# Rotary embedding by heads: a later first store, later reloads, and two-row products on GpSimd

## The chip, the core and the metric

The kernel runs on one core of one Trainium2 chip. The metric is device time in microseconds (us): the median of several executions. One more execution is taken with the hardware profiler; its rows carry every duration used below.

## The reference, cut to what matters

```python
x: (16, 512, 1024) fp32 -> reshape (batch, seq, 16 heads, 64)
x1, x2 = x[..., :32], x[..., 32:]
rotated = concatenate([x1 * cos - x2 * sin, x1 * sin + x2 * cos], axis=-1)   # cos, sin: (512, 32)
```

The input is 33.6 MB and the output is 33.6 MB; each element of x is read once and each element of the result is written once.

## The kernel before

**Rows and tiles.** One "row" is 128 partitions by 1024 fp32 elements (16 heads of 64), that is 0.5 MB. The work has 64 rows, numbered u = 0 to 63, in ten tiles: tiles 0 and 1 of four rows, tiles 2 to 7 of eight rows, tiles 8 and 9 of four rows. A tile is loaded by one DMA and stored by one DMA. With four rows a partition's piece of it is 16 KB in one stretch, with eight rows 32 KB.

**Per row.** out = x·[cos, cos] + swap(x)·[−sin, sin], where swap exchanges the two halves of every head. The first product, t1, is made by VectorE into PSUM (`mul`, L293; three buffers, `NT1`). The second, t2, is made by GpSimd into SBUF (L257; six buffers, `NT2`). For row 3 of each eight-row tile (`V2`) VectorE makes t2 too (L286). The sum goes back over x in SBUF. VectorE makes it (`comb`, L304) for most rows. For the rows in `PE2` (21 of 64: rows 1, 3 and 6 of an eight-row tile, one or two in the four-row tiles) TensorE adds t2 to t1 in PSUM by a product with the identity (L224), and ScalarE copies the sum to x (L191).

**Order.** Every engine's program is written out by hand, in row order. VectorE's loop does `mul(u)` and then `comb(u-1)`. At one place, the test called `ahead`, it does `comb(u-1)` first: before, at u = 4, so that the sum of row 3 (the last of tile 0) comes before the product of row 4. A `mul` waits until the t1 buffer of row u−3 is free; GpSimd waits until the t2 buffer of row u−6 is free.

**Transfers.** x has a ring of 40 rows (`RING`). ScalarE's queue issues all loads (L153): those of tiles 0 to 5 at once, at the start. Tiles 6, 7 and the pair 8 and 9 reuse ring places. Each waits on ScalarE for the store that empties its place (`sem_out`), and stands in ScalarE's program behind a certain row: behind row 7 + `LAG` = 17 for tile 6, row 25 for tile 7, row 33 for tiles 8 and 9. While ScalarE waits there it can't copy any sum. SyncE issues the stores (L161) in tile order, each after `wait_added` for the tile's last row: all VectorE sums and ScalarE copies up to that row.

Of the kernel before, what the change touches and what calls it, by code (L numbers as in the profile page):

```python
# [6 lines left out]
def bass_split_heads_rope_kernel(  # L7
# [17 lines left out]
    H = int(num_heads)  # L25
    HD = dim // H
    HALF = HD // 2
    P = 128
    R1 = seq // P
    R2 = 2 * R1  # L30
# [4 lines left out]
    mult = mybir.AluOpType.mult  # L35
# [5 lines left out]
    tiles = [(b, R1 if b in singles else R2) for b in range(batch) if b in singles or b % 2 == 0]  # L41
# [3 lines left out]
    rows = [(t, r) for t, (_, n) in enumerate(tiles) for r in range(n)]  # L45
    NU = len(rows)
# [1 line left out]


    V_ROW = 3  # L50
    PE2 = [R1 <= u < NU - R1 and u % R2 in (1, 3, 6) for u in range(NU)]
    V2 = [tiles[t][1] == R2 and r == V_ROW for t, r in rows]

    def count(flags):
        return [sum(flags[: u + 1]) for u in range(NU)]

    n_pool = count([not v for v in V2])
    n_pe = count(PE2)
    n_comb = count([not a for a in PE2])

    NT1 = 3
    NT2 = 6
    BANK = 512
    EH = H * HD // BANK
    LEAD = 1
    LAG = 10

    with ExitStack() as stack:
        x_sb = stack.enter_context(nc.sbuf_tensor([P, RING, H, 2, HALF], fp32))
        t2_sb = stack.enter_context(nc.sbuf_tensor([P, NT2, H, 2, HALF], fp32))  # L70
        stage = stack.enter_context(nc.sbuf_tensor([P, 2, R1 * HALF], fp32))
        s1_sb = stack.enter_context(nc.sbuf_tensor([P, R1, 2, HALF], fp32))
        s2_sb = stack.enter_context(nc.sbuf_tensor([P, R2, 2, HALF], fp32))
# [16 lines left out]
        sem_p = stack.enter_context(nc.semaphore("pool"))  # L90
# [10 lines left out]
        def c_of(t, r):  # L101
            return c1_ps[:, r, :] if tiles[t][1] == R1 else pair_ps[:, r // R1, 0, r % R1, :]

        def s_of(t, r):
            return s1_sb[:, r] if tiles[t][1] == R1 else s2_sb[:, r]
# [7 lines left out]
        def in_dram(single, pairs, t):  # L113
            b, n = tiles[t]
            return single[b] if n == R1 else pairs[b // 2]

        def in_sbuf(t):
            b, n = tiles[t]
            k = b * R1 % RING
            return x_sb[:, k:k + n].rearrange("p n h t d -> p (n h t d)")  # L120

        def where(u):
            t, r = rows[u]
            return t, r, u % RING

        def swapped(k):
            return x_sb[:, k, :, ::-1, :]

        def over_heads(table):
            return table[:, None, :, :].broadcast_to([P, H, 2, HALF])  # L130

        def wait_added(eng, u):

            if n_pe[u]:
                eng.wait_ge(sem_a, n_pe[u])
            if n_comb[u]:
                eng.wait_ge(sem_v, n_comb[u])  # L137

        def wait_t2_free(eng, u):

            if u >= NT2:
                v = u - NT2
                if PE2[v]:
                    eng.wait_ge(sem_e, n_pe[v])
                else:
                    eng.wait_ge(sem_v, n_comb[v])

        def stores_of(k):

            return sum(b * R1 // R2 == k for b, _ in tiles)  # L150
# [4 lines left out]
        def on_sync(sp):  # L155
            for u in range(NU):
                t, r, k = where(u)
                if r == tiles[t][1] - 1:
                    wait_added(sp, u)
                    k = u // R2  # L160
                    sp.dma_start(in_dram(o1, o2, t), in_sbuf(t)).then_inc(sem_out[k] if k < EARLY else sem_rest, 16)  # L161
            sp.wait_ge(sem_rest, 16 * sum(stores_of(k) for k in range(EARLY, NU // R2)))

        def on_scalar(ae):
            later = {}
            for t, (b, n) in enumerate(tiles):
                if b * R1 + n <= RING:
                    load(ae, t)
                else:

                    later.setdefault((b * R1 - RING) // R2 * R2 + R2 - 1 + LAG, []).append(t)
                if t == 0:
# [15 lines left out]
            for u in range(NU):  # L188
                if PE2[u]:
                    ae.wait_ge(sem_e, n_pe[u])  # L190
# [6 lines left out]
        def on_tensor(pe):  # L197
# [17 lines left out]
            for u in range(NU):  # L215
                if not PE2[u]:
                    continue
# [16 lines left out]
        def on_gpsimd(pl):  # L234
            pl.memset(ident[:], 1.0).then_inc(sem_i, 1)  # L235
            pl.wait_ge(sem_i, 1)
            pl.affine_select(  # L237
                out=ident[:],
                in_=ident[:],
                compare_op=mybir.AluOpType.is_equal,  # L240
                fill=0.0,
                base=0,
                pattern=[[-1, P]],
                channel_multiplier=1,
            ).then_inc(sem_i, 1)
            for u in range(NU):
                if V2[u]:
                    continue
                t, r, k = where(u)
                if (t, r) == (0, 0):  # L250
                    pl.wait_ge(sem_s, 1)
                if (t, r) == (2, 0):
                    pl.wait_ge(sem_s, 2)
                if r == 0:
                    pl.wait_ge(sem_in[t], 16)
                wait_t2_free(pl, u)
                pl.tensor_tensor(  # L257
                    t2_sb[:, u % NT2, :, :, :], swapped(k), over_heads(s_of(t, r)), mult
                ).then_inc(sem_p, 1)

        def on_vector(ve):
            ve.memset(zero[:], 0.0).then_inc(sem_z, 1)  # L262
            ve.wait_ge(sem_cos, 16)
            ve.tensor_copy(c1_ps, stage[:, 0, :].rearrange("s (r d) -> s r d", d=HALF)).then_inc(sem_c, 1)  # L264
            ve.wait_ge(sem_c, 1)
            ve.wait_ge(sem_w, NT1 * EH)

            def pair_tables():
                ve.wait_ge(sem_s, 2)
                row = pair_ps[:, V_ROW // R1, 1, V_ROW % R1, :]  # L270
                ve.tensor_scalar_mul(v_ps[:, 0, :], row, -1.0).then_inc(sem_c, 1)
                ve.tensor_copy(v_ps[:, 1, :], row).then_inc(sem_c, 1)

            first_v = V2.index(True)

            def mul(u):
                t, r, k = where(u)
                if r == 0:
                    ve.wait_ge(sem_in[t], 16)
                if (t, r) == (2, 0):  # L280
                    pair_tables()
                if u == first_v:
                    ve.wait_ge(sem_c, 3)
                if V2[u]:
                    wait_t2_free(ve, u)
                    ve.tensor_tensor(t2_sb[:, u % NT2, :, :, :], swapped(k), over_heads(v_ps), mult)  # L286
                if u >= NT1:
                    v = u - NT1
                    if PE2[v]:
                        ve.wait_ge(sem_a, n_pe[v])  # L290
                    else:
                        ve.wait_ge(sem_v, n_comb[v])
                ve.tensor_tensor(  # L293
                    t1_ps[:, u % NT1, :].rearrange("p (h d) -> p h d", d=HALF),
                    x_sb[:, k, :, :, :].rearrange("p h t d -> p (h t) d"),
                    c_of(t, r)[:, None, :].broadcast_to([P, 2 * H, HALF]),
                    mult,
                ).then_inc(sem_m, 1)

            def comb(u):  # L300
                t, r, k = where(u)
                ve.wait_ge(sem_m, u + 1)
                ve.wait_ge(sem_p, n_pool[u])  # L303
                ve.tensor_tensor(  # L304
                    xs[:, k, :],
                    t1_ps[:, u % NT1, :],
                    t2_sb[:, u % NT2, :, :, :].rearrange("p h t d -> p (h t d)"),
                    add,
                ).then_inc(sem_v, 1)

            for u in range(NU + LEAD):

                ahead = u == R1
                if ahead:
                    comb(u - LEAD)
                if u < NU:
                    mul(u)
                if u >= LEAD and not ahead and not PE2[u - LEAD]:
                    comb(u - LEAD)

        on_sync(nc.sync)
        on_scalar(nc.scalar)
        on_gpsimd(nc.gpsimd)
        on_tensor(nc.tensor)
        on_vector(nc.vector)


# [31 lines left out]
```

## Time and profile before

| what | value |
|---|---|
| median of 3 runs | 161.26 us (161.24 to 161.27) |
| profiled execution, its own time | 161.16 us |
| its span in the profile | 159.8 us |
| DMA traffic in it | 67.26 MB, mean 421 GB/s |
| GpSimd busy | 134.9 us (84%), 58 products of 2350 ns |
| VectorE busy | 130.1 us (81%) |
| TensorE busy / ScalarE busy | 70.4 us / 24.4 us |

The page gives the busy time of each engine, the span in 40 slices, the DMA queues (q10 carries the loads, q1 the stores), the chain of work that ended last, and groups of instructions by line. Program names appear without their numbers: `t_ps` is t1, `t_sb` is t2. The span is 1.36 us shorter than the profiled execution's own time.

### The profile page before, as it was taken

The page shows a single profiled execution, that of the slowest core. Times are in us where ns is not written, and L with a number is a line of the kernel's source. Part 1 is how long each engine was busy: PE and PEld are TensorE (multiplying, and loading weights), DVE is VectorE, ACT ScalarE, POOL GpSimd, SP SyncE. Part 2 cuts the span into 40 slices and gives each one's busy share as a digit, 9 for nine tenths or more (in the row PEclk, how much of TensorE's full clock was granted, in tenths as well). Part 3 has the DMA queues.
Part 4 walks back from the last instruction along what each step waited for, and adds up shares of the span by engine and source line. Part 5 has one row for each costly group of instructions (what it writes and reads, how often), then busy time and mean ns, then how long its engine had stood idle before and what let it go on. Part 6 is the DMA issues. An engine that isn't in the chain of part 4 may idle for free.

```text
span 159.8 us, 522 instructions
## 1 busy us (share of the span) xinstructions
PE 70.4 (44%) x94; PEld 22.9 (14%) x94; DVE 130.1 (81%) x117; ACT 24.4 (15%) x27; POOL 134.9 (84%) x64
## 2 busy tenths in 40 slices
PE   6050005376437731680943505468439842970000
PEld 1020002021202210220211002012202210320000
DVE  0069799699999999996989809999999989989600
ACT  0420000205020502022022010220220122050000
POOL 1069999999999999999999999698999999289400
PEclk9999999969855899567599675855855595577555
DMA  5999999999999999999999999999999999999997
GB/s 144 404 453 476 402 410 435 439 468 406 402 451 435 462 410 402 492 410 410 443 443 427 410 459 435 402 459 398 429 443 439 451 406 423 476 410 443 402 431 299
DMA packets 3170, 67.26 MB, mean 421 GB/s; under 512 B 352, under 2 KB 608, under 8 KB 608
## 3 DMA queue, kind: packets, MB, share of 16 engines
q10 hardware_dynamic: 1728, 33.69, 49.6%
q1 hardware_dynamic: 1440, 33.56, 48.8%
q14 instruction: 2, 0.02, 0.0%
HBM read 33.69 MB, written 33.55 MB: 421 GB/s over the span
## 4 chain that ended last, share of the span: by engine, by line
DMA 60%; POOL 28%; issue 3%; DVE 2%; ACTq 1%; DVEq 0%; SPq 0%
DMA x_sb<-in_x_dram 41%; POOL t_sb L257 28%; DMA out_dram<-x_sb 19%; DVE x_sb L304 1%; ACTq L153 1%; DVE t_ps L293 1%; ACTq L174 1%; DVEq L303 0%; SPq L137 0%
## 5 line engine op out<-in xcount | busy, mean ns | idle before, releaser
L257 POOL TENSOR_TENSOR t_sb<-x_sb,s_sb 128x1024 f32<-128x1024 f32 x58 | 134.2, 2350 | 14.1 <-ACT s_sb L183 8.1
L224 PE MATMUL t_ps<-t_sb,ident 128*128 128x512 f32 x84 | 65.6, 933 | 65.9 <-DVE t_ps L293 39.5
L293 DVE TENSOR_TENSOR t_ps<-x_sb,pair_ps 128x1024 f32<-128x1024 f32 x48 | 57.7, 1223 | 9.5 <-ACT x_sb L191 9.5
L304 DVE TENSOR_TENSOR x_sb<-t_ps,t_sb 128x1024 f32<-128x1024 f32 x43 | 52.4, 1219 | 2.0 <-POOL t_sb L257 2.0
L191 ACT ACTIVATE x_sb<-t_ps 128x1024 f32<-128x1024 f32 x21 | 21.5, 1023 | 110.4 <-PE t_ps L224 96.8
L224 PEld LDWEIGHTS t_ps<-t_sb,ident 128*128 128x128 f32 x84 | 21.0, 276 | 110.2 <-DVE t_ps L293 66.4
L293 DVE TENSOR_TENSOR t_ps<-x_sb,tab_ps 128x1024 f32<-128x1024 f32 x16 | 19.2, 1222 | 0.5 <-ACT x_sb L191 0.5
L286 DVE TENSOR_TENSOR t_sb<-x_sb,tab_ps 128x1024 f32<-128x1024 f32 x6 | 7.3, 1216 | 0.0
L264 DVE COPY tab_ps<-stage 128x128 f32<-128x128 f32 x1 | 0.3, 295 | 7.9 <-DMA stage<-in_cos_dram 7.9
L208 PE MATMUL pair_ps<-stage,pick 128*128 128x256 f32 x4 | 2.0, 667 | 5.1 <-DMA stage<-in_cos_dram 5.1
L201 PE MATMUL t_ps<-zero 128*128 128x512 bf16 x6 | 2.7, 630 | 1.3 <-DVE zero L262 1.3
L208 PEld LDWEIGHTS pair_ps<-stage,pick 128*128 128x128 f32 x4 | 1.2, 326 | 6.2 <-issue 6.0
L177 ACT ACT_TABLE_LOAD x1 | 1.3, 1283 | 5.1 <-issue 5.1
L201 PEld LDWEIGHTS t_ps<-zero 128*128 128x128 bf16 x6 | 0.7, 137 | 2.4 <-DVE zero L262 1.2
L262 DVE MEMSET zero<- 128x256 uint32 x1 | 0.3, 272 | 0.9 <-PEq L341 0.9
L186 ACT ACTIVATE s_sb<-pair_ps 128x256 f32<-128x256 f32 x1 | 0.4, 383 | 1.8 <-PE pair_ps L208 1.8
L182 ACT ACTIVATE s_sb<-stage 128x128 f32<-128x128 f32 x1 | 0.3, 309 | 2.1 <-DMA stage<-in_sin_dram 2.1
L235 POOL MEMSET ident<- 128x128 f32 x1 | 0.2, 205 | 0.3 <-POOLq L341 0.3
L177 ACT ACTIVATE pick<-ident 128x256 f32<-128x256 f32 x1 | 0.4, 429 | 0.0
L187 ACT ACTIVATE s_sb<-pair_ps 128x256 f32<-128x256 f32 x1 | 0.4, 378 | 0.0
L237 POOL TENSOR_SCALAR_AFFINE_SELECT ident<-ident 128x128 f32<-128x128 f32 x1 | 0.3, 294 | 0.1
L341 POOL MEMSET const-float32-0.0<- 128x1 f32 x1 | 0.1, 100 | 0.3 <-issue 0.3
(6 smaller groups left out, 1.0 us busy)
## 6 DMA issues: line engine op xcount, KB each, us to landing
x_sb<-in_x_dram ACTq DMA_DIRECT2D x6, 4096.0 KB, 37.9
out_dram<-x_sb SPq DMA_DIRECT2D x6, 4096.0 KB, 25.4
x_sb<-in_x_dram ACTq DMA_DIRECT2D x4, 2048.0 KB, 22.3
out_dram<-x_sb SPq DMA_DIRECT2D x4, 2048.0 KB, 14.9
stage<-in_sin_dram ACTq DMA_DIRECT2D x1, 64.0 KB, 7.7
stage<-in_cos_dram ACTq DMA_DIRECT2D x1, 64.0 KB, 7.4
```

Source lines behind the costliest of these rows:

```text
L153: eng.dma_start(in_sbuf(t), in_dram(x1, x2, t)).then_inc(sem_in[t], 16)
L174: ae.dma_start(stage[:, i, :], table.rearrange("(s r) d -> s (r d)", r=R1)).then_inc(sem, 16)
L177: ae.activation(pick[:], ident[:].rearrange("q (s k) -> q k s", k=2)[:, :, None, :].broadcast_to([P, 2, 2, P // 2]), COPY).then_inc(sem_g, 1)
L186: ae.activation(s2[:, :, :, 0, :], pair_ps[:, :, 1, :, :], COPY, scale=-1.0)
L191: ae.activation(xs[:, u % RING, :], t1_ps[:, u % NT1, :], COPY).then_inc(sem_a, 1)
L201: pe.matmul(t1_ps[:, k, b * BANK:(b + 1) * BANK], zero[:, 0:P], zero[:], start=True, stop=True).then_inc(sem_w, 1)
L208: pe.matmul(pair_ps[:, k].rearrange("p c r d -> p (c r d)"), pick[:, k].rearrange("q b s -> q (b s)"), stage[:].rearrange("q c f -> q (c f)"),
L224: ins = pe.matmul(t1_ps[:, u % NT1, b * BANK:(b + 1) * BANK], ident[:], t2[:, b * BANK:(b + 1) * BANK], start=False, stop=True, skip_group ...
L257: pl.tensor_tensor(t2_sb[:, u % NT2, :, :, :], swapped(k), over_heads(s_of(t, r)), mult).then_inc(sem_p, 1)
L286: ve.tensor_tensor(t2_sb[:, u % NT2, :, :, :], swapped(k), over_heads(v_ps), mult)
L293: ve.tensor_tensor(t1_ps[:, u % NT1, :].rearrange("p (h d) -> p h d", d=HALF), x_sb[:, k, :, :, :].rearrange("p h t d -> p (h t) d"), c_of ...
L304: ve.tensor_tensor(xs[:, k, :], t1_ps[:, u % NT1, :], t2_sb[:, u % NT2, :, :, :].rearrange("p h t d -> p (h t d)"), add,).then_inc(sem_v, 1)
```

## The change

Four things change together.

1. Tile 0's store waits for one row more (`HOLD = 1`): for the sum of row 4, which belongs to tile 1. In VectorE's loop the place where a sum comes ahead of the product moves by one row too: the sum of row 4 is made before the product of row 5.
2. `LAG` goes from 10 to 16: the loads of tiles 6, 7 and 8/9 stand behind rows 23, 31 and 39 in ScalarE's program.
3. In eight-row tiles GpSimd makes the t2 products of rows 0 and 1, 4 and 5, 6 and 7 by one instruction each (`TWO`); row 2 stays single and row 3 stays with VectorE. A pair waits for both of its t2 buffers and signals once, at its end.
4. In eight-row tiles TensorE's third row is row 5 instead of row 6.

```diff
-    PE2 = [R1 <= u < NU - R1 and u % R2 in (1, 3, 6) for u in range(NU)]
+    PE2 = [R1 <= u < NU - R1 and u % R2 in ((1, 3, 6) if u < R2 else (1, 3, 5)) for u in range(NU)]
...
-    n_pool = count([not v for v in V2])
+    TWO = [tiles[t][1] == R2 and r in (0, 4, 6) for t, r in rows]
+    n_pool = count([not V2[u] and not (u and TWO[u - 1]) for u in range(NU)])
...
-    LAG = 10
+    LAG = 16
+    HOLD = 1
...
-                    wait_added(sp, u)
+                    wait_added(sp, u + HOLD if t == 0 else u)
...
-                if V2[u]:
+                if V2[u] or (u and TWO[u - 1]):
                     continue
...
-                wait_t2_free(pl, u)
-                pl.tensor_tensor(
-                    t2_sb[:, u % NT2, :, :, :], swapped(k), over_heads(s_of(t, r)), mult
-                ).then_inc(sem_p, 1)
+                m = 2 if TWO[u] else 1
+                for v in range(u, u + m):
+                    if v == u + m - 1 or PE2[v - NT2] != PE2[v + 1 - NT2]:
+                        wait_t2_free(pl, v)
+                if m == 1:
+                    pl.tensor_tensor(
+                        t2_sb[:, u % NT2, :, :, :], swapped(k), over_heads(s_of(t, r)), mult
+                    ).then_inc(sem_p, 1)
+                else:
+                    table = s1_sb if tiles[t][1] == R1 else s2_sb
+                    pl.tensor_tensor(
+                        t2_sb[:, u % NT2:u % NT2 + 2].rearrange("p n h t d -> p (n h) t d"),
+                        x_sb[:, k:k + 2, :, ::-1, :].rearrange("p n h t d -> p (n h) t d"),
+                        table[:, r:r + 2].rearrange("p n t d -> p n (t d)")[:, :, None, :].broadcast_to(
+                            [P, 2, H, HD]
+                        ),
+                        mult,
+                    ).then_inc(sem_p, 1)
...
-                ahead = u == R1
+                ahead = u == R1 + HOLD
```

## The prediction

> **What bounds the kernel now.** I read the page's slices and queues first, then busy time by stage, then the end of the chain of waits.
>
> The slices of the span (tenths busy; GB/s moved) and the two DMA queues:
>
> ```profile
> DMA  5999999999999999999999999999999999999997
> GB/s 144 404 453 476 402 410 435 439 468 406 402 451 435 462 410 402 492 410 410 443 443 427 410 459 435 402 459 398 429 443 439 451 406 423 476 410 443 402 431 299
> q10 hardware_dynamic: 1728, 33.69, 49.6%
> q1 hardware_dynamic: 1440, 33.56, 48.8%
> ```
>
> The transfer engines are full in every slice but the first and last. The queues' shares add to 98.4% of 159.8 us = 157.2 us; 2.6 us are left, at the start (first packets 1.8 us in) and the end. Loads and stores are each made once, so this is all traffic there is. Is the rate the same whatever is mixed? Busy time by stage (the last two columns are DMA share and GB/s):
>
> ```profile
> 4.00:20.00 16.00, 2.05 (x4) 1.18 (x4) 9.63 (x9) 2.88 (x6) 10.52 (x5) 1.00 1.02 433
> 60.00:100.00 40.00, 18.39 (x25) 6.19 (x24) 33.06 (x30) 6.14 (x6) 39.62 (x18) 0.71 1.00 433
> 100.00:140.00 40.00, 24.85 (x31) 7.55 (x30) 39.05 (x35) 7.32 (x8) 34.77 (x15) 0.63 1.01 433
> ```
>
> Loads alone (4 to 20) run at 433 GB/s, and so do the half-and-half mix and the store-heavy one. The time is traffic over a fixed rate, plus the ends, as long as no moment has both queues empty. The only place where that can happen is the end, so the chain's last pieces and the last three stores (KB, us from issue to landing) matter:
>
> ```profile
> 93.30 47.00 DMA x_sb<-in_x_dram
> 140.30 0.07 issue
> 140.37 9.29 POOL t_sb L257 x4
> ...
> 149.75 1.23 DVE x_sb L304
> ```
>
> ```profile
> out_dram<-x_sb SPq DMA_DIRECT2D x1, 4096.0 KB, 15.1
> out_dram<-x_sb SPq DMA_DIRECT2D x1, 2048.0 KB, 11.1
> out_dram<-x_sb SPq DMA_DIRECT2D x1, 2048.0 KB, 8.7
> ```
>
> The three stores were issued at 134.9, 143.8 and 151.1, so they land at 150.0, 154.9 and 159.8. The chain names GpSimd for 28%, but the last store then queues behind its predecessor from 151.1 to 154.9: the chain's 9.29 us of GpSimd do not set the end. About 1 us passes from issue to first packet (loads: issued 0.8, moving at 1.8), so the last store could be issued at 153.9 without a gap: 2.8 us of slack.
>
> **The change part by part.** GpSimd's program, the engine that paces all sums:
>
> ```profile
> 9.48 90.14 POOL L257 TENSOR_TENSOR t_sb<-x_sb,s_sb 128x1024 f32<-128x1024 f32 x39 [8.11 <-ACT s_sb L183]
> 101.29 9.29 POOL L257 TENSOR_TENSOR t_sb<-x_sb,s_sb 128x1024 f32<-128x1024 f32 x4 [1.67 <-PE t_ps L224]
> 111.29 25.48 POOL L257 TENSOR_TENSOR t_sb<-x_sb,s_sb 128x1024 f32<-128x1024 f32 x11 [0.70 <-DMA x_sb<-in_x_dram]
> 140.37 9.29 POOL L257 TENSOR_TENSOR t_sb<-x_sb,s_sb 128x1024 f32<-128x1024 f32 x4 [3.60 <-DMA x_sb<-in_x_dram]
> ```
>
> *First store.* It goes out behind VectorE's sum of row 3:
>
> ```profile
> 18.87 1.23 DVE L304 TENSOR_TENSOR x_sb<-t_ps,t_sb 128x1024 f32<-128x1024 f32 x1 [1.08 <-POOL t_sb L257]
> ...
> 20.12 0.38 SPq L161 DMA_DIRECT2D out_dram<-x_sb  x1
> 22.27 1.22 DVE L304 TENSOR_TENSOR x_sb<-t_ps,t_sb 128x1024 f32<-128x1024 f32 x1
> ```
>
> Now it waits for row 4's sum. GpSimd starts a product every 2.31 us (90.14 / 39); its fifth ends at 9.48 + 4 × 2.31 + 2.35 = 21.1, the sum takes 1.22, so the store leaves at about 22.4, 2.3 us later. Behind it on SyncE is only tile 1's store, not due until 30.6. The loads of tiles 2 to 5 are queued then and take the 2.3 us at the same 433 GB/s, so the cost is nothing. Without that cover it would be 2.3 us. What follows: the stream of stores is shifted by 2.3 us; as the two queues share about half and half from then on, the loads come some 2.3 us earlier, the last one at about 138.0 instead of 140.3. No engine waits for tile 1's data there, and the product of row 5 moves behind one sum of 1.13 us, while GpSimd stays the pacer.
>
> *Reloads.* Tile 6's load now stands behind row 21's copy (the last TensorE row before 23), tile 7's behind row 29's, tiles 8 and 9's behind row 37's: at about 60, 77 and 93 us from the row times of before, instead of 53.9, 73.5 and 92.9. Tile 2's store then lands at 73.5 + 2.3 = 75.8, before 77. Tile 3's lands at 92.9 + 2.3 = 95.2, so ScalarE still waits 2 us, but its next copy (row 41) is not due before 97. What goes is this stall:
>
> ```profile
> 92.92 2.16 ACTq L153 DMA_DIRECT2D x_sb<-in_x_dram  x2
> 95.12 1.02 ACT L191 ACTIVATE x_sb<-t_ps 128x1024 f32<-128x1024 f32 x1 [9.70 <-issue]
> 96.18 1.23 DVE L293 TENSOR_TENSOR t_ps<-x_sb,pair_ps 128x1024 f32<-128x1024 f32 x1 [4.80 <-ACT x_sb L191]
> ```
>
> The 4.8 us of VectorE, 1.45 us at 73.9 and GpSimd's 1.67 us at 101.3 go. They are worth nothing in the end, since GpSimd then waits for data anyway: it would begin tile 7 after 8 + 35 products, at 9.48 + 43 × 2.31 = 108.8, when that load lands at 111.2 − 2.3 = 108.9. Is the load queue ever empty? The loads ahead of these three land at 72.5 (issued 4.5, the longest at 68.0 us), 53.9 + 38.0 = 91.9 and 73.5 + 37.7 = 111.2, less 2.3 in the new order: 10 us and more behind the issues. Cost nothing; even a dry load queue leaves stores to move, and would be paid only from the slack at the end.
>
> *Pairs.* 36 products become 18. No row shows a GpSimd product of 2048 elements. GpSimd's smallest instructions take 0.1 us (memset of one element per partition), so one instruction less saves at most that: the lower bound is 2 × 2.31 − 0.1 = 4.52 us. Two full durations are 4.70. The operand has one more dimension, whose cost no row shows; VectorE's products cost the same with quite different operands (1216, 1222, 1219 ns), so I take 4.62 and keep 5.3 (15% more) as the far end. [...]
>
> *What pairs delay.* The first row of a pair is ready 2.3 us later. The stretch of seven products and VectorE's 14 instructions per tile are 16.2 us and 14 × 1.13 = 15.9 us, so VectorE has little to spare. TensorE's row takes 2.1 us from product to copy at full clock and 3.9 us at half. With rows 1, 3 and 5 one after the other, at half clock throughout, I get 16.8 us per tile (4.5 us from row 1's product to row 3's, two TensorE rows of 3.9, a copy of 1.1, then row 0's product, row 7's sum and row 1's product at 1.13 each). Rows 1, 3 and 6 give about the same. At worst that is 0.6 × 6 = 3.6 us.
>
> *The end.* The last load at 138.0, then four single products and the last sum as before (10.8 us from landing to issue, 140.3 to 151.1): the last store leaves at 148.8, and the one before it lands at 154.9. Slack grows from 2.8 to 5.1 us. GpSimd, if it never waits, reaches the last four rows at 108.8 + 25.4 = 134.2; it may be as late as 153.9 − 10.7 = 143.2. So 9.0 us of lost compute time are covered: 18 pairs of up to 4.62 + 0.50 = 5.1 us, or the 3.6 us of TensorE.
>
> Sum: 0 + 0 + 0. Span 159.8, own time 161.16; the median of before lies 0.10 above it. I forecast 161.2. A difference under 0.2% (0.3 us) is about what a measurement of this kernel can't tell from none.
>
> **Rivals.**
>
> *Slower: the pair is dear.* If the two-row product costs over 5.1 us, GpSimd reaches the last four rows after 143.2 and both queues run dry at the end. At 5.3 us: 18 × 0.68 = 12.2 us lost, 9.0 covered, 3.2 us slower: 164.4; at 5.17 about 162.1. For it: a form that the trace doesn't have, on the engine that paces the sums. Against: it must be 10% over two single products. Chance 0.13.
>
> *Slower: the queue order.* If the later reloads leave the load queue dry for some 5 us, the stores take its place, the last load lands after 138.0 + 5.1 = 143.1 and the slack is gone: each us beyond costs one, 162 to 163. Against: 10 us of queued loads at each reissue. Chance 0.06.
>
> *Faster: the rate.* The stages reach 433 GB/s, while 4 to 156 us as a whole moved 65.57 MB at 431. If the new order took the whole at 433, that is 0.7 us: 160.5. For it: the first store enters after tile 2's load is further on. Against: three stages of different mix have one rate. [...] Chance 0.11.
>
> **How the numbers follow.** No difference: 0.70; slower 0.13 + 0.06 = 0.19; faster 0.11. The forecast's own range is 160.95 to 161.55. Reaching into both sides, to 160.7 and to 162.2 (a pair of 5.17 us, or a load late by 1 us), leaves out less than 2 in 10.
>
> **What would show it.** Right: DMA slices full from second to last but one, shares near 98.4%, first store at 22.4, ScalarE's 9.7 us before L191 gone, last load near 138, last store issued near 149 and landing 10 us or more after. The pair's row near 4.6 us. Wrong: a slice under 9 before the last, a pair over 5.1 us, or the last store landing some 6 us after its issue, which would mean that it found the queue empty.

## The result, and the profile after

| | before | changed |
|---|---|---|
| median (13 runs each) | 161.24 us | 161.46 us |
| ratio of the runs | | 1.0017, 95% interval 1.0009 to 1.0024 |
| span of the profiled execution | 159.8 us | 160.1 us |

The changed kernel is 0.17% slower: 0.27 us by the ratio, 0.22 us between the two medians. That is inside the 0.2% that the prediction called no difference, but the interval excludes 1, and the forecast time lay a little below before. So the question is a small one: where do 0.3 us come from, when almost everything else came out as worked out?

Slices and queues of the changed kernel:

```profile
DMA  5999998999999999999999999998999999999896
GB/s 147 413 451 463 409 475 360 430 414 450 446 409 442 457 409 409 483 418 401 442 459 409 401 500 409 401 483 377 479 414 405 446 416 471 426 409 467 385 430 291
q10 hardware_dynamic: 1728, 33.69, 49.9%
q1 hardware_dynamic: 1440, 33.56, 48.7%
```

Three slices between the first and the last have 8 in place of 9: the seventh (24 to 28 us, 360 GB/s), the 28th (108 to 112 us, 377 GB/s; 398 before) and the 38th (148 to 152 us, 385 GB/s; 402 before). The prediction had named a slice under 9 as a sign of being wrong. But these digits count a packet where it begins. With each packet's time shared out over the slices that it spans, the engines are busy throughout in all three, and the rates are 417, 432 and 431 GB/s (429, 431 and 432 before). So the engines are full to the end, and of the three only the seventh slice moved clearly less than before: it is the one to follow. The loads' queue now takes 49.9% of 160.1 = 79.9 us, against 49.6% of 159.8 = 79.3 us before, for the same bytes; the stores' takes 78.0 us in both. By stage (DMA share and GB/s last):

```profile
4.00:20.00 16.00, 2.05 (x4) 1.18 (x4) 10.67 (x10) 2.88 (x6) 10.46 (x5) 1.00 1.02 432
60.00:100.00 40.00, 20.09 (x27) 7.11 (x28) 39.59 (x36) 6.61 (x7) 40.00 (x11) 0.73 1.00 433
100.00:140.00 40.00, 23.33 (x30) 7.55 (x28) 35.77 (x32) 8.19 (x8) 33.63 (x11) 0.71 1.01 433
```

The three stages that the prediction read are unchanged within 1 GB/s. The one that it did not use is 20 to 36 us, where the first store runs. Before, and then changed:

```profile
20.00:36.00 16.00, 6.94 (x8) 2.34 (x8) 14.70 (x16) 1.02 (x1) 16.00 (x8) 0.90 1.03 439
```

```profile
20.00:36.00 16.00, 7.11 (x8) 2.35 (x8) 12.97 (x14) 1.02 (x1) 16.00 (x7) 1.00 1.01 422
```

Such a row counts a packet where it begins, so a short stretch is coarse. Summed packet by packet and pro rata, 20 to 36 us moved 6.870 MB before and 6.732 MB after: 0.32 us at 432 GB/s. In that stretch 31 load packets of 32 KB, which take 1.21 us elsewhere, took more than 1.3 us in the changed kernel (up to 1.63), against 6 before (up to 1.64). "Stretched" below means such a packet, and rates and MB without a row beside them are summed packet by packet.

The stretch does not wait for the store's packets. The first store is issued at 22.47 us, the first stretched packets of loads begin at 24.8, and the store's own first packet begins at 26.2. Before, these times are 20.12, 22.2 and 23.9 us. In every profile used here the first stretched load packet begins 1.0 to 2.8 us after the first store's issue, and the store's own first packet 3.7 to 4.1 us after it. So the first store has its stretched packets at its old place too; at its new place there are more of them.

The end of the chain, and the last two stores (KB, us from issue to landing):

```profile
96.28 41.81 DMA x_sb<-in_x_dram
138.09 0.07 issue
138.16 9.28 POOL t_sb L265 x4
...
147.53 1.23 DVE x_sb L322
```

```profile
out_dram<-x_sb SPq DMA_DIRECT2D x1, 2048.0 KB, 16.9
out_dram<-x_sb SPq DMA_DIRECT2D x1, 2048.0 KB, 11.2
```

The last load lands at 138.1, the last two stores are issued at 138.3 and 148.8 and land at 155.2 and 160.0. All of it is where the prediction put it (138.0, 148.8, 11 us of waiting in the queue). The first store and GpSimd's program:

```profile
21.21 1.23 DVE L322 TENSOR_TENSOR x_sb<-t_ps,t_sb 128x1024 f32<-128x1024 f32 x1 [1.08 <-POOL t_sb L265]
...
22.47 0.37 SPq L165 DMA_DIRECT2D out_dram<-x_sb  x1
```

```profile
L270 POOL TENSOR_TENSOR t_sb<-x_sb,s_sb 128x2048 f32<-128x2048 f32 x18 | 81.1, 4538 | 2.2 <-DMA x_sb<-in_x_dram 2.2
```

```profile
108.93 4.51 POOL L270 TENSOR_TENSOR t_sb<-x_sb,s_sb 128x2048 f32<-128x2048 f32 x1 [2.15 <-DMA x_sb<-in_x_dram]
...
124.67 9.27 POOL L265 TENSOR_TENSOR t_sb<-x_sb,s_sb 128x1024 f32<-128x1024 f32 x4
138.16 9.27 POOL L265 TENSOR_TENSOR t_sb<-x_sb,s_sb 128x1024 f32<-128x1024 f32 x4 [4.22 <-DMA x_sb<-in_x_dram]
```

A pair takes 4.54 us, and back to back one starts 4.48 us after the other; GpSimd waits for data twice, 2.15 and 4.22 us, so its work is hidden. ScalarE at the reload of tiles 8 and 9:

```profile
91.66 1.02 ACT L195 ACTIVATE x_sb<-t_ps 128x1024 f32<-128x1024 f32 x1 [2.37 <-PE t_ps L228]
95.91 0.88 ACTq L156 DMA_DIRECT2D x_sb<-in_x_dram  x2
101.38 1.02 ACT L195 ACTIVATE x_sb<-t_ps 128x1024 f32<-128x1024 f32 x1 [8.69 <-PE t_ps L228]
```

It still waits for tile 3's store, until 95.9, but its next copy is not ready before 101.4: the stall has gone, and it brought nothing.

### The profile page after: what moved, and what is told of

The parts are those of the page before. It is cut to its first block, busy times and chain, and to the rows that moved or that the text cites. A ratio compares the mean times of both kernels' runs of the same rounds, so it can differ in the third digit from the quotient of the medians.

```text
span 160.1 us, 511 instructions
## 1 busy us (share of the span) xinstructions
PE 70.8 (44%) x94; PEld 24.1 (15%) x94; DVE 130.1 (81%) x117; ACT 24.4 (15%) x27; POOL 132.2 (83%) x46
## 3 DMA queue, kind: packets, MB, share of 16 engines
q10 hardware_dynamic: 1728, 33.69, 49.9%
## 4 chain that ended last, share of the span: by engine, by line
DMA 59%; DVE 13%; POOL 11%; PE 5%; issue 2%; ACTq 1%; ACT 1%; DVEq 0%; SPq 0%
DMA x_sb<-in_x_dram 39%; DMA out_dram<-x_sb 20%; POOL t_sb L265 9%; DVE t_ps L311 7%; PE t_ps L228 5%; DVE x_sb L322 5%; POOL t_sb L270 3%; DVE t_sb L304 2%; ACT x_sb L195 1%; ACTq L156 1%; ACTq L178 1%; DVEq L321 0%; DVEq L308 0%; SPq L140 0%
## 5 line engine op out<-in xcount | busy, mean ns | idle before, releaser
L270 POOL TENSOR_TENSOR t_sb<-x_sb,s_sb 128x2048 f32<-128x2048 f32 x18 | 81.1, 4538 | 2.2 <-DMA x_sb<-in_x_dram 2.2
L265 POOL TENSOR_TENSOR t_sb<-x_sb,s_sb 128x1024 f32<-128x1024 f32 x22 | 51.2, 2356 | 12.4 <-ACT s_sb L187 8.2
L228 PEld LDWEIGHTS t_ps<-t_sb,ident 128*128 128x128 f32 x84 | 22.2, 292 | 103.6 <-DVE t_ps L311 69.5
```

The costliest lines, as they stand in the source:

```text
L228: ins = pe.matmul(t1_ps[:, u % NT1, b * BANK:(b + 1) * BANK], ident[:], t2[:, b * BANK:(b + 1) * BANK], start=False, stop=True, skip_group ...
L265: pl.tensor_tensor(t2_sb[:, u % NT2, :, :, :], swapped(k), over_heads(s_of(t, r)), mult).then_inc(sem_p, 1)
L270: pl.tensor_tensor(t2_sb[:, u % NT2:u % NT2 + 2].rearrange("p n h t d -> p (n h) t d"), x_sb[:, k:k + 2, :, ::-1, :].rearrange("p n h t d ...
```

## The experiments

The theories: A, the later first store costs; B, the pairs cost; C, the later reloads cost; D, it is chance. Ratios stand against before, beside runs on the same chip, with 95% intervals. They come from 11 or 12 runs of each kernel, where no other number is given.

**One part at a time.**

Later first store alone:

```diff
+    HOLD = 1
...
-                    wait_added(sp, u)
+                    wait_added(sp, u + HOLD if t == 0 else u)
...
-                ahead = u == R1
+                ahead = u == R1 + HOLD
```

> Before, with the first store's wait and VectorE's moved sum alone. Theory A (the later first store costs: beside it, from 24 to 36 us, load packets stretch, and in the changed kernel that stretch moved 0.4 us less than before): slower by 0.2 to 0.3 us, with the loss between 24 and 36 us. Theory B (the two-row products cost) and theory C (the later reloads cost): no difference, within 0.1 us. Theory D (chance of single executions): no difference over five rounds.

Measured: 1.0002 (0.9991 to 1.0014). Between 20 and 36 us it moved 6.774 MB, 0.22 us behind before: the loss is there, the time is not. (At 140 us this profile is 0.06 us behind before.)

Later reloads alone (`LAG = 16`):

> Before, with LAG = 16 alone. A, B and D: no difference, within 0.1 us, though ScalarE's 9.7 us wait before tile 8's load is gone. C: slower by 0.2 to 0.3 us, with DMA time lost after 54 us, where the first of the later reloads stood.

Measured: 0.9999 (0.9988 to 1.0011). C falls, within the interval. ScalarE's 9.7 us stall was worth nothing.

Pairs and TensorE's row 5 alone (the changed kernel with `LAG = 10`, `HOLD = 0`):

> Before, with the two-row products and TensorE's row 5 instead of 6 alone; first store and reloads as before. A, C and D: no difference, within 0.1 us, pairs at 4.54 us. B: slower by 0.2 to 0.3 us, and load packets stretch between 28 and 36 us.

Measured: 1.0017 (1.0002 to 1.0032), with 6.830 MB from 20 to 36 us. This spoke for B, but it did not hold: see below.

The changed kernel with the first store at its old place (`HOLD = 0`):

> The changed kernel with the first store at its old place (20.1 us). A: the loss is gone, as before within 0.1 us, and 24 to 36 us moves as much as before. B, C: the loss stays, 0.2 to 0.3 us slower than before. D: no difference.

Measured: 1.0004 (0.9991 to 1.0018), and 6.833 MB from 20 to 36 us. As A wants it.

**The whole again, and doses.**

> The changed kernel once more, on the chip and beside the runs of before that the next three share. Theory A2 (the later first store makes the packets of tile 3's load stretch beside it, 0.1 to 0.2 us, and the rest is the slowest of 16 transfer engines, hit by single stretched packets): slower by 0.1 to 0.3 us, load packets stretched between 24 and 36 us again, as in the two executions that had the later store. Theory B (pairs): slower by 0.2 to 0.3 us too, but where packets stretch need not recur. Theory D (chance): no difference, and 24 to 36 us as before.

Measured: 1.0015 (1.0003 to 1.0028); no profile of it is used, as the profiled execution was one of 297.96 us.

The changed kernel with `LAG = 10`:

> The changed kernel with LAG back at 10: later first store and pairs. A2 and B: as the changed kernel, 0.1 to 0.3 us slower than before; loss between 24 and 36 us by A2. If only all three together cost: no difference.

Measured: 1.0019 (1.0007 to 1.0031), 6.713 MB from 20 to 36 us. The reloads' place does not matter.

The first store held three rows (`HOLD = 3` in its wait, VectorE's order as before):

> Before, with the first store held until row 7's sum (about 29.4 us, 9 us later than before), VectorE's order as before: four times the delay. A2: the stretch follows the store, to 31 us and on, and the total is 0.1 to 0.4 us slower. If the amount of delay counted in itself, four times 0.2 = 0.8 us slower. Theory D: no difference. Either way no empty queue: the loads of tiles 2 to 5 cover the wait.

Measured (4 runs): 1.0121 (1.0105 to 1.0138), 2 us: no theory had that. (The edit waits for the sum of row 6, which ScalarE copies, not of row 7.) Three things were left out.

- The loads. The first store leaves just ahead of tile 1's at 30.5 us, tile 1's lands at 63.0, and at `LAG = 10` ScalarE and with it the reload of tile 6 wait for that until 63. The last load issued before it had landed at 62.3, so no load moved until 67.7 us. Stores filled the engines meanwhile.
- Stretched packets. Between 66.1 and 78.4 us 42 packets of 32 KB, 15 of stores and 27 of loads, took 1.3 to 2.6 us in place of 1.21; a lead of 0.16 us over before at 64 us became a lag of 1.06 us at 80.
- The end. From 140 to 142 us the engines moved 0.37 MB against 0.87 before, which is 1.1 us of empty queues, and another 0.2 us is empty ahead of the last store, at 156 us. These are about the other half of the 2 us: the sums came too late, as in the kernel with two rows of delay below.

Up to 60 us hardly anything stretched (two load packets, at 32 and 34 us), though the store's packets, from 34.6 us on, run beside tile 4's load as the changed kernel's do beside tile 3's. So the stretch does not simply follow the store, and A2 is not right as a rule.

Six more GpSimd products, one in each eight-row tile, into a buffer that nothing reads:

```diff
+    EXTRA = (2, 3, 4, 5, 6, 7)
...
                 if m == 1:
+                    if t in EXTRA:
+                        if EXTRA.index(t):
+                            pl.wait_ge(sem_d, EXTRA.index(t))
+                        pl.tensor_tensor(dead[:], swapped(k), over_heads(s_of(t, r)), mult).then_inc(sem_d, 1)
```

> The changed kernel with one more GpSimd product of row 2 in each of the six eight-row tiles, into a buffer that nothing reads: 6 x 2.31 = 13.9 us more work on GpSimd. If compute is covered until the last store finds the queue empty: five of them delay tile 7's start from 106.8 + 11.6 = 118.3 against 108.9, the sixth makes it 11.7 us at the last four rows, which start at 133.9 + 11.7 = 145.6 against a latest start without a gap of 138.2 + 5.1 = 143.3: 2.3 us slower, with empty transfer slices near 155 us. If GpSimd's time counts in full where the chain of waits names it: 7 to 14 us slower.

Measured (2 runs): 1.0178 (1.0156 to 1.0199), 2.9 us; span 162.6, 2.5 us above the changed kernel's. GpSimd's end, and the last store:

```profile
136.11 18.51 POOL L272 TENSOR_TENSOR t_sb<-x_sb,s_sb 128x1024 f32<-128x1024 f32 x8
...
156.21 0.33 SPq L168 DMA_DIRECT2D out_dram<-x_sb  x1
```

```profile
out_dram<-x_sb SPq DMA_DIRECT2D x1, 2048.0 KB, 6.3
```

Eight products without a wait from 136.1: the last four start at 136.1 + 4 × 2.31 = 145.4 (145.6 expected). The store is issued at 156.2 and lands 6.3 us later: it found the queue empty. Of 13.9 us added, 11.4 were covered, by the 2.5 us of the span. This is the sign that the prediction named for the slower case, and what the changed kernel does not have.

**Two rows of delay; the pairs taken apart.**

> Before, with the first store held until row 5's sum and VectorE's early sum moved to row 5: the store leaves near 24.7 us. The loss between 24 and 36 us was 0.3 to 0.4 us in each execution with the store at 22.5 us and the total of the run with that alone 0.0%. Theory A3 (packets stretch where the first store's packets begin together with a new load, tile 3's at 23.6 us): at 24.7 the store begins in the middle of that load, and 24 to 36 us loses under 0.15 us. Theory A2 (any store beside tile 3's load): it loses 0.3 us again. By either the time stays within 0.15% of before, as long as tile 1's store and the reloads are not late.

Measured: 1.0032 (1.0013 to 1.0050), 6.729 MB from 20 to 36 us: 0.33 us behind before, though the store was issued at 24.65 and its first packet began at 28.7, in the middle of tile 3's load. A3 falls. It had also taken the store's issue for its start: the store's packets begin right behind the start of tile 3's load in the kernel before (23.9 us), and not in the one with the later store (26.2 us). The rest is another matter, the end:

```profile
59.69 1.02 ACT L192 ACTIVATE x_sb<-t_ps 128x1024 f32<-128x1024 f32 x1 [6.02 <-DMA out_dram<-x_sb]
...
153.92 0.33 SPq L162 DMA_DIRECT2D out_dram<-x_sb  x1
```

```profile
out_dram<-x_sb SPq DMA_DIRECT2D x1, 2048.0 KB, 6.3
```

At `LAG = 10` ScalarE waits 6 to 8 us for each store that a reload needs, all sums come later, and the last store finds the queue empty by some half a us. The later reloads would keep this stall away, as they do in the changed kernel; that they would save the time here is not shown, as no run had two rows of delay with `LAG = 16`.

Pairs with TensorE's rows 1, 3, 6; then TensorE's row 5 alone; then pairs and row 5 once more:

> Before, with the two-row products alone, TensorE's rows 1, 3 and 6 as before. Theory B (the two-row products cost what the clock shows: the four comparisons with pairs stand at +0.04 to +0.19%, the two without at 0.0%): slower by 0.1 to 0.2%. Theory B2 (it is the place of TensorE's third row): no difference. Theory D (the scatter of the slowest transfer engine): within 0.1%.

> Before, with TensorE's third row at 5 instead of 6 alone. B and D: no difference, within 0.1%. B2: slower by 0.1 to 0.2%.

> Two-row products and TensorE's row 5 alone, once more. B or B2: slower by 0.1 to 0.2% again (0.17% in the first comparison). D: within 0.1%, and the last engine's lag behind the others, 1.4 us in the first profile, is under 0.6 us in this one.

Measured: 0.9992 (0.9981 to 1.0004), 0.9996 (0.9985 to 1.0008), 0.9998 (0.9974 to 1.0022). B and B2 fall: neither costs by itself. The last profile did not show what D expected, as its last transfer engine ended 0.8 us behind the middle one.

**A part out of the whole, side by side.**

> The changed kernel whole, beside three kernels that each lack a part. All theories: slower than before by 0.1 to 0.2%. A2 (later first store): load packets stretch from 24 to 36 us again, some 0.3 us.

> The changed kernel without the two-row products and with TensorE's row 6: later first store and later reloads. A2: as the whole, 0.1 to 0.2% slower than before. B (pairs) or both together needed: within 0.08% of before.

> The changed kernel without the later first store. A2 or both together needed: within 0.08% of before. B: 0.1 to 0.2% slower.

> Before with the later first store alone, once more (0.02% in the first comparison). A2: 0.1 to 0.2% slower. Both together needed: within 0.08% of before.

Measured: the whole 1.0014 (1.0004 to 1.0025); without the pairs 1.0008 (0.9996 to 1.0021); without the later store 0.9999 (0.9989 to 1.0010); the later store alone 1.0008 (0.9995 to 1.0021). All comparisons together:

| kernels | ratios less 1, in % | MB from 20 to 36 us |
|---|---|---|
| later store and pairs | 0.17, 0.15, 0.19, 0.14 | 6.732, –, 6.713, 6.779 |
| later store, no pairs | 0.02, 0.08, 0.08 | 6.774, 6.718, 6.731 |
| pairs, store at its old place | 0.17, 0.04, −0.08, −0.02, −0.01 | 6.830, 6.833, 6.831, 6.746, 6.878 |
| neither (later reloads; row 5) | −0.01, −0.04 | 6.824, 6.872 |

The means are 0.16, 0.06, 0.02 and −0.02%. Without the later store no difference is left; with it the loss from 20 to 36 us is in every profile (6.71 to 6.78 MB, against 6.82 to 6.88 in all but one of the others, and 6.870 before). Not in the table are the kernels with three or two rows of delay, with extra products, and the two that follow.

**The place of the second code fetch.** Two 8 KB transfers of instructions stand in most of the traces (309 ns each). The first comes at 54 to 61 us everywhere. The second comes at GpSimd's 65th recorded instruction or near it (62nd to 69th): at 106 to 120 us without pairs, at 129 to 139 us with the changed kernel's pairs, where GpSimd has fewer instructions (46 on the page against 64). In the profiles of before and of the changed kernel 65 of GpSimd's recorded instructions, waits among them, start ahead of it, at 114.3 and 132.0 us. One kernel puts a one-element memset ahead of each pair, the other uses pairs in the four-row tiles too, with the first store at its old place:

```diff
+                    pl.memset(dead[:, u:u + 1], 0.0)
                     table = s1_sb if tiles[t][1] == R1 else s2_sb
```

```diff
-    TWO = [tiles[t][1] == R2 and r in (0, 4, 6) for t, r in rows]
+    TWO = [r in ((0, 4, 6) if tiles[t][1] == R2 else (0, 2)) for t, r in rows]
...
-    HOLD = 1
+    HOLD = 0
```

> The changed kernel with a one-element GpSimd memset ahead of each of the 18 pairs (0.1 us each, under GpSimd's slack), so that GpSimd's instruction count is as before. Theory F (the place of the second instruction fetch makes the last transfer engine late): fetch back at 106 to 119 us, the last engine under 0.7 us behind the middle one, and the time within 0.08% of before. If the fetch is not it: 0.14 to 0.19% slower as the changed kernel, wherever the fetch stands.

> Pairs in the four-row tiles too, the first store at its old place, reloads 16 rows behind: GpSimd's program is eight instructions shorter, ends under the 65, and the second fetch should not come at all. F: the last engine has one transfer of 0.3 us less, and the time is 0 to 0.2% below before. If the fetch is not it: within 0.1% of before. The last store leaves some 0.7 us later than in the kernel before, inside its 2.8 us of slack.

Measured: the first 1.0011 (1.0002 to 1.0020), with the fetch back at 104.4 us and the last engine 0.6 us behind the middle one: the place of the fetch is not it, or not all of it. The second (6 runs) has no second fetch and is 1.0102 (1.0082 to 1.0121), 1.5 us slower by the medians. Its last store left at 152.1, inside the slack, and its engines stay full up to 159 us, so compute is not the reason. By stage, and one row of before beneath it:

```profile
64.00:72.00 8.00, 5.73 (x7) 2.09 (x8) 8.00 (x8) 1.02 (x1) 8.00 (x3) 0.53 1.02 438
72.00:80.00 8.00, 4.09 (x7) 1.31 (x5) 7.59 (x8) 2.05 (x2) 8.00 (x3) 0.71 0.99 393
```

```profile
72.00:80.00 8.00, 3.78 (x4) 1.18 (x4) 6.55 (x7) 1.02 (x1) 8.00 (x4) 0.61 1.02 438
```

From 72 to 80 us the engines are full in both, and move 393 GB/s by the row against 438; packet by packet it is 400 against 433. Between 72.5 and 75.4 us seventeen load packets took 1.47 to 2.09 us in place of 1.21. No transfer was issued between 64.4 and 76.1 us, so this burst does not stand behind an issue. At 64 us this kernel was level with before, at 80 us 0.60 us behind, at 140 us 0.88 us. The other half us of its profile comes at the end, where the last transfer engine is 1.3 us behind the middle one, against 0.4 before.

## Why the prediction was right or wrong

**Right, by its own steps.** The first store at 22.47 (22.4 forecast), the last load at 138.1 (138.0), the last store at 148.8 and 11.2 us in the queue, ScalarE's stall gone without a gain. The slack rule was put to the test by the six extra products: 2.3 us expected, 2.5 in the span. The pair was a term sized a little high. The 4.62 us of the prediction are twice the distance between two starts (2.31), so they compare with 4.48 us from start to start and not with the 4.54 us that a pair is busy; 4.48 is even under the lower bound of 4.52. That makes 18 × 0.14 = 2.5 us less work for GpSimd (busy 132.2 us against 134.9), all of it hidden.

**Wrong: the step that failed** is the one on the first store: the loads "take the 2.3 us at the same 433 GB/s, so the cost is nothing". The 2.3 us themselves were filled. From 20 to 24 us the changed kernel even gained 0.08 us, as the stretched packets of before lie there. But then, behind the store's issue and beside its packets, more load packets stretched, and from 20 to 36 us the eight profiles with the store at its new place moved 0.09 MB or 0.2 us less on average than the nine with it at its old place or near it. Part is given back: from 36 to 140 us these kernels, all but the one with the extra products, gain 0.1 to 0.2 us on before, as packets stretch less there. At 140 us these seven are 0.06 to 0.15 us behind before, with pairs or without.

The rest comes at the end. The trace has 16 landings for the last store; they are read here as one for each of the 16 transfer engines. In the changed kernel's profile these come 0.14 us later than before on average (159.38 against 159.24 us), and the last of them 0.31 us later (160.03 against 159.72). By that reading the slower packets are about half of the difference between the two profiles, and the lateness of the last engine is the other half. The prediction had no term for either. In the runs the later store makes the difference: taken out of the whole, it leaves 0.9999 and 1.0004. But alone it gives only 0.06%, not told from nothing, and the measured 0.17% needs the pairs too.

The reading behind that step was that one rate holds whatever is mixed. It came from three stages of 16 to 40 us, none of which holds the stretch from 20 to 36 us where the first store stands, and the rival "the rate" used it in one direction only, as a gain of up to 0.7 us; it went the other way. Nor do the 400 GB/s with full engines from 72 to 80 us in the kernel with pairs everywhere fit one rate: before moved 433 there.

**The forecast's bound.** That 0.2% is "about what a measurement of this kernel can't tell from none" was too wide: 13 runs on each side tell 0.17% from nothing. The forecast was a statement on terms of 2 us and more, and had none for tenths.

**Open.** Why the pairs, which cost nothing alone, add to the later store's loss. The four comparisons with both average 0.1% above the three with the later store and no pairs, and the intervals of the two groups overlap. A trace of a cause is at the end: the last transfer engine ends 0.6 to 1.6 us behind the middle one in the nine profiles with pairs and TensorE's row 5 (the one with the extra products apart), and 0.15 to 0.7 us behind it in the seven others that end in transfers (before, later reloads, row 5 alone, pairs with row 6, and the three with the later store and no pairs); yet pairs alone did not time slower, and moving the code fetch did not settle it. This trace is weak: in the four profiles with pairs and row 5 and the store at its old place (0.8 to 1.6 us) the profiled execution itself took 0.3 to 1.0 us more than the median of its kernel's runs. Nor was it tried why packets stretch. The traces show where they do, often 1 to 3 us behind the issue of a transfer of the other direction, but not always, and not which part of the memory path is behind it. No version was found that beats the kernel before by more than its interval.

## What to carry to other kernels

Here the transfer engines were full from start to end (their queues' shares added to 98.4% of the span before), and compute time was worth nothing until the last store found its queue empty: of 13.9 us of added products 11.4 cost nothing. In a kernel with such engines, work out first how much lost compute time is covered (9 us by the sum here); what showed it used up was a last store that landed 6.3 us after its issue, against 11.2 in the changed kernel. Order still mattered a little: full engines did not move at one rate (411 to 434 GB/s in slices of 4 us between 20 and 140 us of the changed kernel), and a store moved by 2 us cost 0.2 us in the stretch where it meets the loads, of which 0.06 to 0.15 us was left at the end of the loads. Read the rate packet by packet, as a view that counts a packet where it begins shows dips that are not there (377 GB/s in the 28th slice, where the packets moved 432). Read it in the stretch where the change moves a transfer, not in the averages around it, and do not call the rate fixed in one direction only.

## What the runs showed of the hardware that was not expected

- A 32 KB packet took 1.21 us nearly everywhere, with 16 engines running, loads or stores or both: up to 1.25 us in 97% of the 1536 such packets before and in 96% in the changed kernel. In bursts of 2 to 10 us packets took 1.3 to 2.2 us (one 2.6), while the engines stayed busy: 411 to 422 GB/s in slices of 4 us from 24 to 36 us in the changed kernel, 400 from 72 to 80 us in the kernel with pairs everywhere and 359 from 76 to 80 us with three rows of delay, where before moved 429 to 433.
- Such a burst of load packets began 1.0 to 2.8 us after the first store's issue in the profiles used here, while the store's own first packet came 3.7 to 4.1 us after it. With three rows of delay, store packets stretched from 3.1 us after the issue of a load whose first packet came 4.7 us after it. In the kernel with two rows of delay the last store, issued at 153.9 us, found the queue empty and began 0.8 us later.
- The last of the 16 landings at the end, read as the slowest of 16 transfer engines, came 0.15 to 1.6 us behind the middle one in the 16 profiles compared (0.4 before, 0.8 in the changed kernel).
- A GpSimd product of 2048 elements took 4.54 us, and the next one started 4.48 us after it did: 0.14 us less than two of 1024, started 2.31 us apart.
